# Four query projections and four gates of a retention layer by seven products, with sums kept in PSUM

## The chip, the cores and the metric

The kernel runs on one core of one Trainium2 chip. The metric is device time in microseconds of one execution, the median of several runs. A profiled execution comes with a trace of every engine: TensorE (PE, with weight loads as PEld), VectorE (DVE), ScalarE (ACT), GpSimd (POOL), and SyncE (SP), which issues most DMAs.

## The reference

One layer of a decoder for 512 tokens and 16 learned meta tokens of width 1024: retention (4 heads, keys of 256, values of 512) and stick-breaking attention (16 heads of 64) from one projection, gated and merged, then a SwiGLU feed-forward network (FFN) of width 2816. All inputs are float32.

```python
proj = hn @ w_in
rq, rk, rv, rg, sq, sk, sv, ga, gb = jnp.split(proj, ...)
q_r = rotary(heads(rq, RET_HEADS), pos) * (RET_DK ** -0.5)
k_r = rotary(heads(rk, RET_HEADS), pos)
y_ret = head_groupnorm(retention_chunkwise(q_r, k_r, heads(rv, RET_HEADS)))
y_ret = (jax.nn.silu(rg) * merge_heads(y_ret)) @ w_ret_out
y_sb = merge_heads(stick_breaking(...)) @ w_sb_out
merged = jax.nn.sigmoid(ga) * y_ret + jax.nn.sigmoid(gb) * y_sb
h = h + rmsnorm(merged @ w_out)
a, b = jnp.split(rmsnorm(h) @ w_ffn_in, 2, axis=-1)
h = h + rmsnorm((jax.nn.silu(a) * b) @ w_ffn_out)
```

## The kernel before

**Number format.** Every operand of a product is split in two parts of the format float32r: `split` copies the rounded high part on ACT (line 104) and subtracts it from the source on DVE for the low part (line 101). A product is then three matmuls per block of 128 inputs: high by high, high by low, low by high. All matmuls are issued through `mm` (line 95), so the profile shows them under one line and they are told apart by their tiles. `hT` and `hL` are the two parts of the normalised, turned input; `wh` and `wl` those of a weight.

**Plain products.** `feat_units` (137) loads blocks of weights (1024 inputs by 128 features) and `feat_mm` (142) multiplies them: features on the partitions, tokens along the columns, 8 x 3 matmuls of 512 columns for one block. Loads go through `raw_of` (118) into four buffers `raw`; the parts lie in five pairs of buffers `wh`, `wl` (pool `wun`).

**Products by seven.** A product of two 2 x 2 block matrices can be made with seven block products in place of eight (the Strassen-Winograd scheme). The class `Tokens` (174) holds the four quarters of the input, b11 to b22, and four sums of them, t1 to t4 (tiles `th`, `tl`). `feat_quarters` (221) and `tok_quarters` (238) load a weight, make its sums s1 to s4 on POOL in tiles `st` (lines 230 and 247 to 258), and split them: `raw1` holds a11 and a12, `x` holds s2 and s3, `y` holds s1 and s4. `seven` (263) runs the products in the order a11·b11, a12·b21, s2·t2, s3·t3, s1·t1, s4·b22, a22·t4, each in a PSUM bank of its own, and adds the results on DVE in a tile `ub` in SBUF (lines 274, 277, 280, 285; the copy of line 269 is on ACT). `feat_seven` (features on the partitions, 12 matmuls of 256 columns a product) serves the FFN: 20 sets of seven after the first two column blocks, on `nT`, `nL`. `tok_seven` (tokens on the partitions, 24 matmuls of 256 columns a product) serves retention's values (`rv_proj`) and its output gate (`ret_gate`).

**PSUM.** There are eight banks of 512 columns: two tiles `pp` (`bank_p`), two `pb` (`bank_b`) and two `pa` (`bank_a`, of two banks each).

**Stages.** The attention stage with the stick-breaking heads comes first, then its output projection, then retention (from about 331 us), one head after another: `ret_qk` makes queries (plain, 2 blocks, both in one `pa` tile) and keys (two blocks, 528 columns in two pieces of 264, each block in a `pa` tile) and rotates them on DVE and ACT; `ret_scores` makes decayed scores; `ret_gate` the output gate; `ret_pv` multiplies scores by values and normalises on DVE; `ret_T` turns the result; `rv_proj` makes the next head's values; `ret_out` multiplies by `w_ret_out` and adds up in `acc`. After the last head the eight blocks of the branch gate `ga` are handled: the first three were made earlier and are loaded, blocks 3 to 7 are plain products here (line 1141), with a sigmoid (1142). `mb` is the other branch, loaded from DRAM (1128); lines 1132 and 1133 multiply `acc` by the gate and add `mb`. The tiles of `ga` lie in the space of the values, `vh` and `vl`. After the output projection (`w_out`) and the norms comes the FFN, from about 852 us, and its second product, from about 1053 us.

**Order.** In most of the kernel the order of instructions on each engine is laid out when the kernel is built, by a planner that follows a model of the times and takes what is ready, in the order of the program's text where several are. So the text below gives priorities rather than an exact order. On the chip each engine then runs its own list in order. A tile with one buffer (`ub`) makes its next user wait until the last reader is done.

Of the kernel before, what the change touches and what calls it, by code (L numbers as in the profile page):

```python
# [16 lines left out]
P = 128  # L17
NM = 16
T = 512
# [15 lines left out]
def hybrid_block(  # L35
# [105 lines left out]

    def feat_mm(dst, unit, xh, xl, kn=KD):

        wh, wl = unit
        for k in range(kn):
            mm(dst, wh[:, k, :], xh(k), start=(k == 0), stop=False)
            mm(dst, wh[:, k, :], xl(k), start=False, stop=False)
            mm(dst, wl[:, k, :], xh(k), start=False, stop=(k == kn - 1))

    def tok_mm(dst, units, xh, xl, first=True, last=True, k0=0):  # L150

        n = sum(u[0].shape[1] for u in units)
        i = 0
        for wh, wl in units:
            for kk in range(wh.shape[1]):
                k = k0 + i
                mm(dst, xh(k), wh[:, kk, :], start=(first and i == 0), stop=False)
                mm(dst, xh(k), wl[:, kk, :], start=False, stop=False)
                i += 1
                mm(dst, xl(k), wh[:, kk, :], start=False, stop=(last and i == n))  # L160

# [59 lines left out]
    def feat_quarters(src, sums, pin=False):  # L221

        raw1, raw2 = raw_of(src[:, 0:P]), raw_of(src[:, P:])
        A11, A12 = raw1[:, 0:KH, :], raw1[:, KH:KD, :]
        A21, A22 = raw2[:, 0:KH, :], raw2[:, KH:KD, :]
        x = sums.tile([P, KD, P], F32, tag="st", name="st")
        y = sums.tile([P, KD, P], F32, tag="st", name="st")
        S1, S2, S3, S4 = y[:, 0:KH, :], x[:, 0:KH, :], x[:, KH:KD, :], y[:, KH:KD, :]
        for d, p, q, op in ((S1, A21, A22, ALU.add), (S2, S1, A11, ALU.subtract), (S3, A11, A21, ALU.subtract), (S4, A12, S2, ALU.subtract)):
            ins = nc.gpsimd.tensor_tensor(d, p, q, op=op)  # L230
            if pin:
                tc.keep_in_program_order(ins)
        f, g = slice(0, KH), slice(KH, KD)
        a, b, c, d = wun_split(raw1), wun_split(x), wun_split(y), wun_split(A22)
        cut = lambda u, k: (u[0][:, k, :], u[1][:, k, :])
        return dict(a11=cut(a, f), a12=cut(a, g), s2=cut(b, f), s3=cut(b, g), s1=cut(c, f), s4=cut(c, g), a22=d)

    def tok_quarters(src, sums=None):
# [17 lines left out]
        for d, p, q, op in ((y, A11, A21, ALU.subtract), (A21, A21, A22, ALU.add), (x, A21, A11, ALU.subtract), (A12, A12, x, ALU.subtract)):  # L256
            for k in range(0, KH, 2):
                nc.gpsimd.tensor_tensor(d[:, k : k + 2], p[:, k : k + 2], q[:, k : k + 2], op=op)  # L258
        u["s2"], u["s3"], u["s1"] = wun_split(x), wun_split(y), wun_split(A21)
        u["s4"], u["a22"] = wun_split(A12), wun_split(A22)  # L260
# [35 lines left out]

    def tok_seven(u, tok, ub, **kw):


        def product(n, dst):  # L300
            a, b = PRODUCTS[n]
            xh, xl = tok.operand(b)
            wh, wl = u[a]
            for s in range(2):
                ts_ = slice(s * P, (s + 1) * P)
                tok_mm(dst[:, s * 256 : (s + 1) * 256], [(wh, wl)], lambda k: xh(k)[:, ts_], lambda k: xl(k)[:, ts_])

        one = iter([bank_p, bank_p, bank_b])
        seven(product, lambda: next(one)(), bank_a, ub, **kw)

# [610 lines left out]
    s4.tile([P, L], F32, tag="dec", name="dec", bufs=1)  # L921
    s4.tile([P, 4, 512], F32, tag="ub", name="ub", bufs=1)
    s4.tile([P, NT, DV], F32, tag="g", name="g", bufs=1)
# [19 lines left out]
    def rv_proj(h):  # L943
        u = tok_quarters(w_in[:, O_RV + DV * h : O_RV + DV * (h + 1)], s4 if h else None)
        ub = s4.tile([P, 4, 512], F32, tag="ub", name="ub", bufs=1)
        vs = s4.tile([P, L], F32, tag="rt", name="vs", bufs=RT)[:NM, :DV]
# [12 lines left out]

        tok_seven(u, tokens, ub, after=meta_part)  # L960
        vh = s4.tile([P, NT, DV], F32R, tag="vh", name="vh", bufs=1)
        vl = s4.tile([P, NT, DV], F32R, tag="vl", name="vl", bufs=1)
        for q in range(4):
            c, t = q // 2, q % 2
            dst = lambda v: v[:, 2 * t : 2 * t + 2, 256 * c : 256 * (c + 1)]
            split(dst(vh), dst(vl), ub[:, q, :].rearrange("p (a b) -> p a b", a=2))
        split(rvm[0:16, :], rvm[64:80, :], vs)
# [22 lines left out]
    def ret_qk(h):  # L990
        uq = feat_units(w_in[:, O_RQ + DK * h : O_RQ + DK * (h + 1)])
        pq = bank_a()
        for e in range(2):
            feat_mm(pq[:, e, :], uq[e], xtok, ltok)
        q = [(qk_tile(), qk_tile()) for _ in range(2)]
        idf = lambda t: t[:, :T]
        rotate(pq[:, 0, :], pq[:, 1, :], cosT[:, NM:], sinT[:, NM:], idf, [(a[:, :T], b[:, :T]) for a, b in q])
        uk = feat_units(w_in[:, O_RK + DK * h : O_RK + DK * (h + 1)])
        pks = []
        for e in range(2):  # L1000
            pk = bank_a()
            for i in range(2):
                cs = slice(264 * i, 264 * (i + 1))
                feat_mm(pk[:, i, :264], uk[e], lambda k: hT[:, k, cs], lambda k: hL[:, k, cs])
            pks.append(pk[:, :, :264])
        k = [(qk_tile(), qk_tile()) for _ in range(2)]
# [65 lines left out]
    def ret_gate(u):  # L1072
        ub = s4.tile([P, 4, 512], F32, tag="ub", name="ub", bufs=1)
        tok_seven(u, tokens, ub)
        g = s4.tile([P, NT, DV], F32, tag="g", name="g", bufs=1)
        for q in range(4):
            c, t = q // 2, q % 2
            dst = g[:, 2 * t : 2 * t + 2, 256 * c : 256 * (c + 1)]
            nc.scalar.activation(dst, ub[:, q, :].rearrange("p (a b) -> p a b", a=2), AF.Silu)
        return [g[:, i, :] for i in range(NT)]  # L1080
# [30 lines left out]
    for h in range(RH):  # L1111
# [9 lines left out]
        else:  # L1121

            gall = [s4.tile([P, 4, T], F32, tag=t, name="ga", bufs=1) for t in ("vh", "vl")]
            ga = [gall[f // 4][:, f % 4, :] for f in range(KD)]
            base = []
            for f in range(0, KD, 2):
                mb = s4.tile([P, 2, T], F32, tag="st", name="mb")
                nc.sync.dma_start(mb, mS_d[:, f : f + 2, :])
                base += [mb[:, 0, :], mb[:, 1, :]]

# [260 lines left out]
```

## Time and profile before

| | us |
|---|---|
| median of 3 runs | 1178.63 (1178.5 to 1179.28) |
| the profiled execution | 1178.72 |
| its span in the trace | 1176.9 |
| TensorE busy | 1164.9 (99%) |
| VectorE busy | 844.0 (72%) |
| ScalarE busy | 532.1 (45%) |
| GpSimd busy | 333.5 (28%) |
| granted TensorE clock, mean | 0.999 |

Times of rows are in microseconds from the start of the span. A row names line, engine, operation, tiles written and read, and a count. Matmuls are pipelined, so one's recorded duration overlaps the next; the distance from one start to the next is what a matmul takes. Idle time in brackets is that of the row's engine just before it, with what ended it.

### The profile page before, as it was taken

What the parts mean: (1) busy time and instruction counts of PE and PEld (TensorE: products, weight loads), DVE (VectorE), ACT (ScalarE), POOL (GpSimd) and SP (SyncE); (2) the same over time, 40 slices, a digit from 0 to 9 for tenths busy, and PEclk for the clock granted to TensorE, in tenths of its full rate; (3) what the DMA queues carried; (4) which work ended last, traced back from release to release, by engine and by line L of the source; (5) the groups of instructions that cost most, each with busy time, mean ns of one, the idle gap of its engine ahead of it and who ended that gap; (6) DMA issues with size and microseconds to landing.
All of it is one profiled execution on the core that took longest, in us unless ns stands there. A gap on an engine that the chain in (4) does not pass through costs nothing.

```text
span 1176.9 us, 18856 instructions
## 1 busy us (share of the span) xinstructions
PE 1164.9 (99%) x7529; PEld 1056.3 (90%) x7529; DVE 844.0 (72%) x1120; ACT 532.1 (45%) x899; POOL 333.5 (28%) x358
## 2 busy tenths in 40 slices
PE   9999999999999999999999999999999999999997
PEld 7988999988899998998899898888999999998886
DVE  7488888888577873786586567767799998773333
ACT  6476666666233434434243334335455444442321
POOL 2021112126644403320240200001356676610000
PEclk9999999999999999999999999999999999999999
DMA  7332122222641323115122434344033333353311
GB/s 235 99 99 74 62 72 64 77 77 92 194 148 60 93 90 114 55 53 154 36 82 82 133 90 134 126 160 126 19 108 108 109 108 108 108 162 101 97 36 72
DMA packets 146536, 118.25 MB, mean 100 GB/s; under 512 B 3832, under 2 KB 135168, under 8 KB 146448
## 3 DMA queue, kind: packets, MB, share of 16 engines
q1 hardware_dynamic: 145856, 115.85, 32.5%
q8 instruction: 59, 0.97, 0.4%
q10 hardware_dynamic: 592, 1.20, 0.3%
q14 instruction: 29, 0.24, 0.1%
HBM read 109.96 MB, written 7.08 MB: 99 GB/s over the span
## 4 chain that ended last, share of the span: by engine, by line
PE 92%; DVE 5%; issue 1%; ACT 1%; DMA 0%; POOL 0%; POOLq 0%; DVEq 0%; ACTq 0%
PE pp L95 41%; PE pb L95 20%; PE pa L95 20%; PE pc L95 5%; PE px L95 3%; PE pb L98 3%; DVE wl L101 1%; DVE sm L603 1%; ACT wh L104 1%; DVE sl L101 0%; DMA ysb<-in_x_dram 0%; DVE al L101 0%; DVE kl L101 0%; DVE qb L101 0%; DVE qa L101 0%
## 5 line engine op out<-in xcount | busy, mean ns | idle before, releaser
L101 DVE TENSOR_TENSOR wl<-raw,wh 128x1024 fp32r<-128x1024 f32 x196 | 260.7, 1338 | 60.3 <-ACT wh L104 59.3
L104 ACT ACTIVATE wh<-raw 128x1024 fp32r<-128x1024 f32 x194 | 195.2, 1014 | 203.4 <-PE pa L95 59.5
L95 PE MATMUL pp<-hT,wh 128*128 128x512 f32 (+1 forms) x304 | 112.0, 369 | 0.0
L95 PE MATMUL pp<-hL,wh 128*128 128x512 f32 (+1 forms) x304 | 107.7, 354 | 0.0
L95 PE MATMUL pp<-hT,wl 128*128 128x512 f32 (+1 forms) x304 | 107.6, 354 | 0.0
L258 POOL TENSOR_TENSOR st<-raw 128x512 f32<-128x512 f32 x28 | 44.4, 1608 | 170.3 <-DMA raw<-in_w_in_dram 170.3
L101 DVE TENSOR_TENSOR wl<-st,wh 128x1024 fp32r<-128x1024 f32 x54 | 75.1, 1392 | 13.1 <-ACT wh L104 12.1
L95 PE MATMUL pp<-qk,wh 128*128 128x512 f32 x256 | 80.1, 394 | 0.0
L230 POOL TENSOR_TENSOR st<-raw 128x512 f32<-128x512 f32 x40 | 61.1, 1528 | 50.3 <-DVE wl L101 50.3
L95 PE MATMUL pp<-wh,hT 128*128 128x256 f32 (+1 forms) x240 | 73.9, 309 | 0.1
L95 PE MATMUL pp<-wl,hT 128*128 128x256 f32 (+1 forms) x240 | 73.0, 305 | 0.7 <-DVE wl L101 0.4
L95 PE MATMUL pp<-wh,hL 128*128 128x256 f32 (+1 forms) x240 | 73.0, 305 | 0.2 <-DVE hL L101 0.2
L104 ACT ACTIVATE wh<-st 128x1024 fp32r<-128x1024 f32 x54 | 56.6, 1056 | 35.6 <-PE pp L95 15.6
L95 PE MATMUL pa<-hL,wh 128*128 128x264 f32 (+1 forms) x208 | 66.2, 318 | 0.0
L95 PE MATMUL pa<-hT,wh 128*128 128x264 f32 (+1 forms) x208 | 66.2, 318 | 0.0
L95 PE MATMUL pa<-hT,wl 128*128 128x264 f32 (+1 forms) x208 | 66.1, 318 | 0.0
L603 DVE TENSOR_TENSOR_SCAN sm<-sm,mask 128x528 f32<-128x528 f32 (+1 forms) x64 | 54.8, 857 | 14.3 <-ACT sm L600 13.5
L95 PEld LDWEIGHTS pp<-hT,wl 128*128 128x128 f32 x304 | 57.2, 188 | 8.4
L613 POOL CAST mg<-sp 128x32 fp32r<-128x32 f32 x32 | 7.5, 233 | 197.6 <-DVE sp L604 153.7
L95 PEld LDWEIGHTS pp<-hT,wh 128*128 128x128 f32 x304 | 57.3, 188 | 5.8
L95 PEld LDWEIGHTS pp<-hL,wh 128*128 128x128 f32 x304 | 57.4, 189 | 5.3
L95 PEld LDWEIGHTS pp<-qk,wh 128*128 128x128 f32 x256 | 47.7, 188 | 10.7
(346 smaller groups left out, 3680.3 us busy)
## 6 DMA issues: line engine op xcount, KB each, us to landing
raw<-in_w_in_dram SPq DMA_DIRECT2D x88, 512.0 KB, 4.2
raw<-in_w_ffn_in_dram SPq DMA_DIRECT2D x44, 512.0 KB, 3.8
raw<-in_w_ffn_out_dram SPq DMA_DIRECT2D x22, 512.0 KB, 3.6
raw<-in_w_ret_out_dram SPq DMA_DIRECT2D x16, 512.0 KB, 3.4
raw<-in_w_sb_out_dram SPq DMA_DIRECT2D x8, 512.0 KB, 3.9
raw<-in_w_out_dram SPq DMA_DIRECT2D x8, 512.0 KB, 4.0
ysb<-in_x_dram SPq DMA_DIRECT2D x4, 512.0 KB, 7.1
gb_d<-go SPq DMA_DIRECT2D x8, 256.0 KB, 2.0
```

What stands on the lines that cost most here:

```text
L95: return keep(nc.tensor.matmul(*args, **kw))
L98: return keep(nc.tensor.transpose(dst, src, idn))
L101: return nc.vector.tensor_tensor(lo, src, hi.bitcast(F32), op=ALU.subtract)
L104: ins = nc.scalar.activation(hi, src, AF.Copy)
L230: ins = nc.gpsimd.tensor_tensor(d, p, q, op=op)
L258: nc.gpsimd.tensor_tensor(d[:, k : k + 2], p[:, k : k + 2], q[:, k : k + 2], op=op)
L603: nc.vector.tensor_tensor_scan(rev, rev, mask[:, r0:][:, ::-1], 0.0, op0=ALU.mult, op1=ALU.max)
L613: nc.gpsimd.tensor_copy(g[:, two, 0:NM], m)
```

## The change

Retention's queries go from two plain blocks to one set of seven in a new function `feat_chain`, with weights from `feat_quarters`; so do the gate blocks 4, 5 and 6, 7, as two sets. `feat_chain` and a rewritten `tok_seven` make the scheme's partial sums in the PSUM banks: a product continues to accumulate in the bank of an earlier one (`first=False`), after the state in between has been copied out on ACT. In `feat_chain` the first product of the keys is placed before the last product of the chain (`beside`). The four results of `tok_seven` are handed on one by one (`done`) instead of together at the end, the last straight from its bank. `ub` has three parts instead of four and also holds the queries and `mb`; the order in which `feat_quarters` and `tok_quarters` split their sums is changed, for the FFN too. The FFN keeps `seven` and `feat_seven`.

```diff
-    def feat_mm(dst, unit, xh, xl, kn=KD):
+    def feat_mm(dst, unit, xh, xl, kn=KD, first=True, **kw):
...
-            mm(dst, wh[:, k, :], xh(k), start=(k == 0), stop=False)
+            mm(dst, wh[:, k, :], xh(k), start=(first and k == 0), stop=False, **kw)
...
# feat_quarters
-        a, b, c, d = wun_split(raw1), wun_split(x), wun_split(y), wun_split(A22)
+        a, c, b, d = wun_split(raw1), wun_split(y), wun_split(x), wun_split(A22)
# tok_quarters
-            u["s2"], u["s3"], u["s1"], u["s4"] = [wun_split(a) for a in (A11, A21, A22, A12)]
+            u["s2"], u["s1"], u["s3"], u["s4"] = [wun_split(a) for a in (A11, A22, A21, A12)]
...
-        u["s2"], u["s3"], u["s1"] = wun_split(x), wun_split(y), wun_split(A21)
+        u["s2"], u["s1"], u["s3"] = wun_split(x), wun_split(A21), wun_split(y)
...
-    def tok_seven(u, tok, ub, **kw):
...
-        one = iter([bank_p, bank_p, bank_b])
-        seven(product, lambda: next(one)(), bank_a, ub, **kw)
+    def tok_seven(u, tok, ub, done, after=lambda n: None):
...
+        q11, q12, q22 = [ub[:, i, :] for i in range(3)]
+        pa = bank_a()[:, 0, :]
+        product(("a11", "b11"), pa)
+        nc.scalar.activation(q11, pa, AF.Copy)
+        pc = bank_p()
+        product(("a12", "b21"), pc, last=True)
+        after(1)
+        add(q11, pc)
+        done(0, 0, q11)
+        product(("s2", "t2"), pa, True)
+        nc.scalar.activation(q12, pa, AF.Copy)
+        pb = bank_p()
+        product(("s1", "t1"), pb)
+        nc.scalar.activation(q22, pb, AF.Copy)
+        product(("s3", "t3"), pa, True)
+        add(q22, pa)
+        done(1, 1, q22)
+        product(("s4", "b22"), pb, True, True)
+        add(q12, pb)
+        done(0, 1, q12)
+        product(("a22", "t4"), pa, True, True)
+        after(6)
+        done(1, 0, pa)
+
+    def feat_chain(u, tok, q, beside):
...
+        (q11, q12), (q21, q22) = [[q[:, e, H * t : H * (t + 1)] for t in range(2)] for e in range(2)]
+        banks["a"] = bank_a()[:, 0, :H]
+        product(("a11", "b11"), "a")
+        nc.scalar.activation(q11, banks["a"], AF.Copy)
+        banks["b"] = bank_p()[:, :H]
+        product(("s1", "t1"), "b")
+        nc.scalar.activation(q22, banks["b"], AF.Copy)
+        banks["c"] = bank_p()[:, :H]
+        product(("a12", "b21"), "c")
+        add(q11, banks["c"])
+        product(("s2", "t2"), "a", True)
+        nc.scalar.activation(q12, banks["a"], AF.Copy)
+        product(("s4", "b22"), "b", True)
+        add(q12, banks["b"])
+        product(("s3", "t3"), "a", True)
+        add(q22, banks["a"])
+        beside()
+        product(("a22", "t4"), "a", True)
+        nc.scalar.activation(q21, banks["a"], AF.Copy)
...
# rv_proj, ret_gate: split or silu of each result is now in done(), called from tok_seven
...
     def ret_qk(h):
-        uq = feat_units(w_in[:, O_RQ + DK * h : O_RQ + DK * (h + 1)])
-        pq = bank_a()
-        for e in range(2):
-            feat_mm(pq[:, e, :], uq[e], xtok, ltok)
+        uq = feat_quarters(w_in[:, O_RQ + DK * h : O_RQ + DK * (h + 1)], s4)
+        uk = feat_units(w_in[:, O_RK + DK * h : O_RK + DK * (h + 1)])
...
+        pq = s4.tile([P, 3, 512], F32, tag="ub", name="ub", bufs=1)
+        feat_chain(uq, tokens, pq, lambda: keys(0))
         q = [(qk_tile(), qk_tile()) for _ in range(2)]
         rotate(pq[:, 0, :], pq[:, 1, :], ...)
-        uk = feat_units(w_in[:, O_RK + DK * h : O_RK + DK * (h + 1)])
...
+        keys(1)
...
# branch gates after the last head
             for f in range(0, KD, 2):
-                mb = s4.tile([P, 2, T], F32, tag="st", name="mb")
+                if f >= 4:
+                    two = gall[f // 4][:, f % 4 : f % 4 + 2, :]
+                    feat_chain(feat_quarters(w_in[:, O_GA + P * f : O_GA + P * (f + 2)], s4), tokens, two, lambda: None)
+                    nc.scalar.activation(two, two, AF.Sigmoid)
+                mb = s4.tile([P, 3, T], F32, tag="ub", name="mb", bufs=1)[:, 0:2, :]
...
-                    else:
+                    elif f < 4:
                         (u,) = feat_units(w_in[:, O_GA + P * e : O_GA + P * (e + 1)])
```

More of the change, by code (lines that the diff above doesn't have):

```diff
@@ L156, in tok_mm @@
                 k = k0 + i
-                mm(dst, xh(k), wh[:, kk, :], start=(first and i == 0), stop=False)
-                mm(dst, xh(k), wl[:, kk, :], start=False, stop=False)
+                mm(dst, xh(k), wh[:, kk, :], start=(first and i == 0), stop=False, **kw)
+                mm(dst, xh(k), wl[:, kk, :], start=False, stop=False, **kw)
                 i += 1
-                mm(dst, xl(k), wh[:, kk, :], start=False, stop=(last and i == n))
+                mm(dst, xl(k), wh[:, kk, :], start=False, stop=(last and i == n), **kw)
     def rstd_of(dst, ss, eps, scale, n=P):
@@ L295, in feat_seven, with product, add @@
         seven(product, lambda: next(one)()[:, :H], lambda: bank_b().rearrange("p (a b) -> p a b", a=2), ub)
-    def tok_seven(u, tok, ub, **kw):
-        def product(n, dst):
-            a, b = PRODUCTS[n]
+    def tok_seven(u, tok, ub, done, after=lambda n: None):
+        def product(name, dst, more=False, last=False):
+            a, b = name
             xh, xl = tok.operand(b)
-            wh, wl = u[a]
             for s in range(2):
                 ts_ = slice(s * P, (s + 1) * P)
-                tok_mm(dst[:, s * 256 : (s + 1) * 256], [(wh, wl)], lambda k: xh(k)[:, ts_], lambda k: xl(k)[:, ts_])
-        one = iter([bank_p, bank_p, bank_b])
-        seven(product, lambda: next(one)(), bank_a, ub, **kw)
+                tok_mm(dst[:, s * 256 : (s + 1) * 256], [u[a]], lambda k: xh(k)[:, ts_], lambda k: xl(k)[:, ts_], first=not more and s == 0, last=True, skip_group_check=True)
+        def add(d, p):
+            nc.vector.tensor_tensor(d, p, d, op=ALU.add)
+        q11, q12, q22 = [ub[:, i, :] for i in range(3)]
[21 more added lines that the diff above has]
+        done(1, 0, pa)
@@ new lines, in feat_chain, with product, add @@
+    def feat_chain(u, tok, q, beside):
+        banks = {}
+        def product(name, bank, more=False):
+            a, b = name
+            feat_mm(banks[bank], u[a], *tok.operand(b), KH, first=not more, skip_group_check=True)
+        def add(d, p):
+            nc.vector.tensor_tensor(d, p, d, op=ALU.add)
+        (q11, q12), (q21, q22) = [[q[:, e, H * t : H * (t + 1)] for t in range(2)] for e in range(2)]
[17 more added lines that the diff above has]
+        nc.scalar.activation(q21, banks["a"], AF.Copy)
@@ L958, in meta_part, with done @@
             nc.vector.tensor_tensor(vs[:, cs], ps[0:16], vs[:, cs], op=ALU.add)
-        tok_seven(u, tokens, ub, after=meta_part)
         vh = s4.tile([P, NT, DV], F32R, tag="vh", name="vh", bufs=1)
         vl = s4.tile([P, NT, DV], F32R, tag="vl", name="vl", bufs=1)
[L963 to L966, printed above, removed]
+        def done(c, t, v):
+            dst = lambda o: o[:, 2 * t : 2 * t + 2, 256 * c : 256 * (c + 1)]
+            split(dst(vh), dst(vl), v.rearrange("p (a b) -> p a b", a=2))
+        tok_seven(u, tokens, ub, done, after=meta_part)
         split(rvm[0:16, :], rvm[64:80, :], vs)
```

37 lines of the change are left out of this document (18 added, 19 removed).

## The prediction

> **What bounds the kernel now.** I read the page's busy table, then the list of what TensorE waited for, then busy time by stage, then the chain that ended last.
>
> ```profile
> PE 1164.9 (99%) x7529; PEld 1056.3 (90%) x7529; DVE 844.0 (72%) x1120; ACT 532.1 (45%) x899; POOL 333.5 (28%) x358
> ...
> PE pb L98 <- DVE al L101: 1.6, 3, 0.7
> PE pp L760 <- DVE zeros L755: 1.5, 1, 1.5
> ...
> core 0: us, PE busy (x) PEld busy (x) DVE busy (x) ACT busy (x) POOL busy (x), PEclk, DMA share, GB/s
> 467.00:571.00 104.00, 103.92 (x690) 94.97 (x689) 73.18 (x94) 37.11 (x50) 25.82 (x20) 1.00 0.28 85
> 675.00:752.00 77.00, 77.00 (x477) 68.64 (x476) 56.81 (x82) 28.47 (x38) 4.75 (x6) 1.00 0.38 120
> 852.00:1053.00 201.00, 201.00 (x1679) 200.62 (x1678) 179.68 (x178) 95.72 (x118) 120.94 (x74) 1.00 0.38 113
> ```
>
> TensorE is never idle: its two longest waits come to 1.6 and 1.5 us in all, and the three stages (retention head 1, the end of head 3, the FFN's sevens) have none worth naming. The granted clock is 1.00 in each. So the time is the issue of matmuls, and removing some shortens it, as long as nothing that was covered comes out. DVE is the second engine: 70% busy in head 1, 89% in the FFN.
>
> What a matmul costs is its distance to the next, which the chain shows in runs.
>
> ```profile
> 355.46 16.96 PE pa L95 x96
> 372.43 1.29 PE pp L95 x11
> 373.72 5.84 PE pa L95 x48
> ...
> 892.15 2.86 PE pb L95 x24
> ...
> 902.17 2.86 PE pb L95 x24
> ```
>
> The run of 96 in head 0 is the query product (48 matmuls of 512 columns) and the first key product (48 of 264); the second key product alone takes 5.84 us. The query product therefore takes 16.96 - 5.84 = 11.12 us, 0.232 us each. In the FFN one product by seven is 7 x 12 = 84 matmuls of 256 columns, and the same place comes round in 902.17 - 892.15 = 10.02 us, 0.119 us each.
>
> **The gross saving.** Four query products and two pairs of gates (features 4, 5 and 6, 7) go from 48 matmuls of 512 columns to 84 of 256: 6 x (11.12 - 10.02) = 6.6 us. The instruction count rises by 6 x 36 = 216. The FFN's pace is the same form (weights stationary, tokens moving), so I take it as it stands.
>
> [...]
>
> **What else each set of seven adds.** Every weight sum and its split is new work on other engines:
>
> ```profile
> L230 POOL TENSOR_TENSOR st<-raw 128x512 f32<-128x512 f32 x40 | 61.1, 1528 | 50.3 <-DVE wl L101 50.3
> L230 POOL TENSOR_TENSOR st<-raw,st 128x512 f32<-128x512 f32 x20 | 44.5, 2227 | 0.0
> L230 POOL TENSOR_TENSOR st<-st,raw 128x512 f32<-128x512 f32 x20 | 26.2, 1311 | 25.8 <-issue 25.7
> L101 DVE TENSOR_TENSOR wl<-st,wh 128x1024 fp32r<-128x1024 f32 x54 | 75.1, 1392 | 13.1 <-ACT wh L104 12.1 <-PE pb L95 0.8
> L104 ACT ACTIVATE wh<-st 128x1024 fp32r<-128x1024 f32 x54 | 56.6, 1056 | 35.6 <-PE pp L95 15.6 <-PE pa L95 15.2 <-POOL st L230 1.8
> L269 ACT ACTIVATE ub<-pp 128x256 f32<-128x256 f32 x20 | 7.5, 375 | 22.7 <-DVE gt L1283 22.7
> L277 DVE TENSOR_TENSOR ub<-pp,ub 128x256 f32<-128x256 f32 x20 | 8.5, 423 | 1.8
> ```
>
> POOL: four sums, (61.1 + 44.5 + 26.2)/20 = 6.6 us, 40 us over six sets, on an engine busy 25.8 of 104 us. Splits: 3.5 units of 1024 instead of 2, so ACT 1.5 x 1.06 and DVE 1.5 x 1.39 us. Evacuation: four ACT copies and three DVE adds of 256, 1.5 and 1.3 us. Against that the eight token products lose DVE work: three adds over 1024 and one over 512 become three over 512 (the last three rows below).
>
> ```profile
> L258 POOL TENSOR_TENSOR st<-raw 128x512 f32<-128x512 f32 x28 | 44.4, 1608 | 170.3 <-DMA raw<-in_w_in_dram 170.3
> ...
> L274 DVE TENSOR_TENSOR ub<-pa,ub 128x1024 f32<-128x1024 f32 x8 | 9.7, 1211 | 0.8 <-PE pa L95 0.8
> L280 DVE TENSOR_TENSOR ub<-pb,ub 128x1024 f32<-128x1024 f32 x8 | 9.7, 1218 | 1.3 <-PE pb L95 0.9
> L285 DVE TENSOR_TENSOR ub<-pb,ub 128x512 f32<-128x512 f32 x20 | 13.6, 682 | 0.2
> ```
>
> That is 8 x (3 x 1.2 + 0.7 - 3 x 0.7) = 18 us less on DVE, about what the six sets add (6 x (2.1 + 1.3) = 20), and two more ACT copies each. None of this is on TensorE's path by itself: it costs nothing while DVE and ACT have the free 30% and 64% of head 1. The bytes loaded do not change: two blocks of 512 KB per query either way. But the first block now stays in its buffer until POOL has used it, so what stands behind it on SP's queue (keys, then the output gate) is loaded later; before, POOL's sums for the token products waited 170.3 us in all for loads (first row) without TensorE waiting, so I take nothing for it.
>
> **The new waits.** A sum kept in a bank must be copied before the next product may add to it.
>
> In the token products each copy has another product of 24 matmuls (2.86 us) in front of it, against an ACT copy of 0.6 us and possibly one 1.06 us split ahead. I take 0, at most 0.3 each.
>
> In the feature chain (s3, t3) waits for the copy of q12 behind one product of 12 (1.43 us), against 0.38 + 1.06 us. The range is 0 to 0.5 us, six times (no gain is possible here or below: there was no wait to lose). Behind the last product in the chain `a`, the second key product wants a third of the two `pa` tiles, so it waits for the copy of q21 too: 0.4 to 1.9 us, four times. What is queued behind on TensorE is everything; but before, the same place was already filled: between the two key products stand the 1.29 us of `pp` (11 matmuls of the output gate's first product) quoted above. I take 0.1 us per chain and 0.2 per key product, 1.4 us; the ends are 0 and 10.6.
>
> The gates have nothing between (s3, t3) and (a22, t4), which must wait for a DVE add of 0.42 us, perhaps behind a split of 1.4: 0.4 to 2 us twice, unless the next pair's first product fills it. And gates are themselves cover, for the last head's value products and turns:
>
> ```profile
> 719.55 4.17 PE pp L95 x18
> 723.72 2.31 PE pb L95 x10
> 726.03 3.02 PE pp L95 x13
> 729.05 2.99 PE pb L95 x13
> 732.04 1.63 PE pp L95 x7
> ...
> 732.08 0.60 ACT L1142 ACTIVATE ga<-pp 128x512 f32<-128x512 f32 x1 [6.42 <-PE pb L95]
> 744.65 1.29 DVE L1133 TENSOR_TENSOR acc<-acc,mb 128x512 f32<-128x512 f32 x2 [1.36 <-DMA mb<-mS_d]
> ```
>
> The `pp` runs are gate products laid between value products, and the first sigmoid waits until the last value product frees the `vh` and `vl` space. The chain writes its first copy there, so until 732 it can do only products that need no copy. Gate 3 (24 x 0.232) and three products of 12 are 9.9 us, where 38 x 0.232 = 8.8 us were used; enough, barely. Afterwards the cover is 2.2 us shorter. I take half of that as lost, 1.1 us; ends 0 and 4. The load of `mb` now has one buffer where it had two, so it waits on SP's queue for the gates before, and weights of the output products queue behind it. DVE waited 1.36 us for it already (last row), off TensorE's path; features 4 to 7 are merged only after four output products of 12 x 0.232 = 2.8 us, so 0.
>
> **The FFN's order.** `feat_quarters` now splits y (s1, s4) before x (s2, s3), and the FFN still uses s2 third and s1 fifth. Here x and y of one seven:
>
> ```profile
> 898.69 0.68 DVE L274 TENSOR_TENSOR ub<-pb,ub 128x512 f32<-128x512 f32 x1
> 899.29 1.21 DVE L101 TENSOR_TENSOR wl<-st,wh 128x1024 fp32r<-128x1024 f32 x1
> 900.43 0.41 DVE L277 TENSOR_TENSOR ub<-pp,ub 128x256 f32<-128x256 f32 x1
> 900.76 2.25 DVE L101 TENSOR_TENSOR wl<-st,wh 128x1024 fp32r<-128x1024 f32 x1
> ...
> 903.44 0.28 PE L95 MATMUL pb<-th,wh 128*128 128x256 f32 x1
> ...
> 908.40 1.06 ACT L104 ACTIVATE wh<-st 128x1024 fp32r<-128x1024 f32 x1 [0.45 <-POOL st L230]
> 910.50 1.46 DVE L101 TENSOR_TENSOR wl<-st,wh 128x1024 fp32r<-128x1024 f32 x1
> ...
> 913.46 0.28 PE L95 MATMUL pb<-th,wh 128*128 128x256 f32 x1
> ```
>
> x was ready at 900.50 for the product at 903.44. In y's place it is ready at 903.01, 0.4 us early; in the next seven 911.96 against 913.46, 1.5 us, and there the second split had waited for POOL's last sum, so x would come another 1.06 us later: 0.4. Two sevens show leads of 0.4; later ones should have more, since the splits of gate rows that also load DVE in the first sevens stop when their buffers are full. With 18 sevens exposed I put the loss between 0 (a lead remains) and 0.5 us each (9 us), and take 1.8: a few tenths in half of them.
>
> **Sum.** -6.6 + 1.4 + 1.1 + 1.8 = -2.3 with every wait at my value; but the order is laid out again for the new work, and gaps of this kind are all filled in the trace before. I count half of the 4.3, and get -4.4. The profiled execution took 1178.72 us (span 1176.9 and 1.8 around it), 0.1 over the median of 1178.63; 1178.7 - 4.4 gives 1174.3. With no wait at all it is 1172.0; the idle time before (3.1 us above) belongs to other stages and stays.
>
> **Rivals.**
> (1) The FFN becomes late: each x arrives about half a microsecond after its product could start. For it speak DVE's 89% and the 0.4 us leads, against it that a waiting TensorE gives the next x time. It is slower from 0.5 us a seven: 18 x 0.5 = 9 against 6.6, 1181; at 0.8, 1186.5. Chance 0.14.
> (2) The saving is swallowed: the chains' waits at their middle (5 us) leave -1.6 or less, 1177 (1176.3 to 1181). For it speaks that head 3 has no other work to lay between. Chance 0.22.
> (3) Weight loading becomes the bound. The row has 94.97 of 104 us in head 1 and 200.62 of 201 in the FFN, and the change moves matmuls from the first form to the second. A load of 128 columns takes 0.188 us; were they not overlapped, 84 would take 15.8 us, 4.7 over 11.12, six times: 28 us slower, 1207. Against it the FFN issues its 84 in 10.02 us. Chance 0.02.
>
> ```profile
> L95 PEld LDWEIGHTS pp<-qk,wh 128*128 128x128 f32 x256 | 47.7, 188 | 10.7
> ```
>
> [...] The pace of the FFN, at a full share, shows the loads overlapping here.
>
> **Numbers.** Forecast case (the saving less small waits, 1171 to 1176.2) 0.62; rival 2 0.22; rivals 1 and 3 0.16. About 0.2%, 2.4 us, is what a measurement can tell from no change. The range 1171 to 1181 leaves out a little at both ends.
>
> **What would show it.** PE x7745, POOL x382 and near 373 us busy, ACT near 560, DVE near 845; query chains 10.0 us long; FFN returns still 10.02 us (rival 1: longer, with PE waiting for DVE wl); waits of PE for ACT at the copies under 0.5 us each. I am wrong if TensorE's own waits pass 4 us in retention and FFN together.

## The result, and the profile after

The changed kernel took 1185.11 us (median of 5, 1182.19 to 1187.24) against 1178.71 us for the kernel before on the same chip: ratio 1.0054, 95% interval 1.0037 to 1.0071, so 6.4 us slower. The forecast was 1174.3 with a range up to 1181. The profiled execution took 1184.84 us with a span of 1183.1, 6.2 over the span before.

The busy table of the changed kernel's page, then its list of what TensorE waited for (total, times, longest):

```profile
PE 1163.0 (98%) x7745; PEld 1064.9 (90%) x7745; DVE 845.9 (72%) x1142; ACT 553.4 (47%) x949; POOL 379.2 (32%) x382
...
PE pa L95 <- DVE rt L1039: 4.4, 4, 2.1
...
PE pb L95 <- DVE wl L101: 1.6, 1, 1.6
...
PE pa L95 <- DVE ub L310: 1.0, 1, 1.0
PE pp L95 <- DVE wl L101: 0.9, 2, 0.5
...
PE pb L98 <- DVE yn L1128: 0.5, 1, 0.5
```

The work is what was forecast (x7745, x382, DVE 846). The first three waits are new, and so are the last one and one of the two that make 0.9 us; the kernel before had the other (0.4 us). None of the new ones is for ScalarE: the copies of the partial sums hold nothing up. One wait for the keys' rotation (L1039) comes in each head, one wait in the FFN, two at the start of retention (at 339.67 and 354.58), and the one for `yn` at 741.97, before a turn of the last head's result.

**The keys.** The longest is in head 1. Three views of the changed kernel around it: TensorE's instructions, the stretches of 4 us (first figures: length, TensorE busy; granted clock third from the end), and the chain that ended last.

```profile
488.12 0.28 PE L95 MATMUL pp<-wh,tl 128*128 128x256 f32 x1
490.54 0.35 PE L95 MATMUL pa<-wh,hT 128*128 128x256 f32 x1 [2.13 <-DVE rt L1039]
```

```profile
488.00:492.00 4.00, 1.87 (x16) 1.70 (x15) 3.92 (x6) 2.03 (x4) 0.61 (x1) 0.98 0.00 2
492.00:496.00 4.00, 4.00 (x19) 3.51 (x19) 3.51 (x6) 2.13 (x4) 0.00 (x0) 0.59 0.47 142
```

```profile
469.02 4.44 DMA raw<-in_w_in_dram
...
473.54 1.07 ACT wh L104
...
475.90 1.12 POOL st L258
...
477.05 1.07 ACT wh L104
...
479.28 2.32 DVE wl L101
481.60 0.60 DVE rt L1035
...
488.15 1.00 DVE qk L101
...
489.78 0.62 DVE rt L1039
...
490.54 4.41 PE pa L95 x24
```

Of the output gate's products two are issued early, into the `pp` banks; the next, a11·b11, goes into a `pa` tile, and that is free only when VectorE has read the keys out of it. From start to start TensorE loses 490.54 - 488.12 - 0.12 = 2.3 us; measured the same way the four heads lose 0.85, 2.3, 1.1 and 0.8, together 5.0. After the wait the granted clock is 0.59 over 4 us: the 24 matmuls take 4.41 us where a product of this size takes 2.86, some 1.6 us more. The chain reads backwards from there: key rotation, query rotation, a weight split of 2.32 us, two copies on ScalarE, a sum on GpSimd, and a load that landed at 473.46. The loads, sums and splits in it are those of the output gate's weights.

Before the change it was VectorE that waited here. VectorE in head 1 of the kernel before:

```profile
475.57 0.69 DVE L984 TENSOR_TENSOR rt<-rt 128x512 f32<-128x512 f32 x1
...
483.62 0.71 DVE L978 TENSOR_TENSOR rt<-pa,sinT 128x528 f32<-128x528 f32 x1 [4.28 <-PE pa L95]
484.25 0.70 DVE L982 TENSOR_TENSOR rt<-pa,sinT 128x528 f32<-128x528 f32 x1
```

The queries' rotation was over at 476.25, VectorE waited 4.28 us for the second key product, and its last read of the first key block began at 484.25. Now that read begins at 489.70, 5.5 us later, while TensorE begins the second key product only 1.9 us later (479.65 against 477.74).

**The FFN.** Busy time from 860 to 1040 us, before and after:

```profile
860.00:1040.00 180.00, 180.00 (x1511) 180.00 (x1510) 162.77 (x159) 83.87 (x103) 116.49 (x72) 1.00 0.36 106
```

```profile
860.00:1040.00 180.00, 178.45 (x1480) 176.88 (x1478) 157.04 (x153) 78.69 (x101) 112.67 (x69) 1.00 0.35 103
```

In the same time TensorE issues 31 matmuls fewer: 31 x 0.119 = 3.7 us. 1.6 of it is the one wait for `wl`; the rest is a new pace, as the chain of the changed kernel shows.

```profile
942.53 2.85 PE pb L95 x24
...
952.70 2.85 PE pb L95 x24
```

A set of seven comes each 10.17 us, where it was 10.02.

**The start of retention.** The chain of the changed kernel ahead of its wait of 1.0 us (start to start 1.15) at 354.58:

```profile
339.64 5.67 DMA raw<-in_w_in_dram
...
345.37 4.85 POOL st L230 x3
...
353.93 0.61 DVE ub L310
```

The query weights land at 345.31, GpSimd makes four sums of them, and the DVE add that frees the bank of a token product stands behind their splits.

The account, from start to start: -6.6 (saving) + 5.0 (keys) + 1.6 (clock) + 3.7 (FFN) + 1.15 and 0.7 (start of retention, at 354.58 and 339.67) + 0.6 (the wait for `yn`) = +6.15, of the 6.2 between the two spans.

### The profile page after: what moved, and what is told of

Same layout as the page of the kernel before. It is cut to its first block, busy times and chain, and to the rows that moved or that the text cites. A ratio compares the mean times of both kernels' runs of the same rounds, so it can differ in the third digit from the quotient of the medians.

```text
span 1183.1 us, 19411 instructions
## 1 busy us (share of the span) xinstructions
PE 1163.0 (98%) x7745; PEld 1064.9 (90%) x7745; DVE 845.9 (72%) x1142; ACT 553.4 (47%) x949; POOL 379.2 (32%) x382
## 4 chain that ended last, share of the span: by engine, by line
PE 81%; DVE 9%; issue 3%; ACT 3%; DMA 2%; POOL 2%; POOLq 0%; DVEq 0%; ACTq 0%
PE pp L95 38%; PE pb L95 18%; PE pa L95 14%; PE pc L95 5%; DVE wl L101 3%; PE px L95 3%; PE pb L98 2%; ACT wh L104 2%; DMA raw<-in_w_in_dram 2%; DVE sm L659 1%; POOL ts L196 1%; POOL st L230 1%; DVE qk L101 1%; DVE rt L1039 0%; DVE rt L1035 0%
## 5 line engine op out<-in xcount | busy, mean ns | idle before, releaser
L230 POOL TENSOR_TENSOR st<-raw 128x512 f32<-128x512 f32 x52 | 81.5, 1570 | 152.6 <-DMA raw<-in_w_in_dram 66.5
L95 PE MATMUL pp<-hT,wh 128*128 128x512 f32 (+2 forms) x320 | 112.9, 353 | 0.0
L95 PE MATMUL pp<-hT,wl 128*128 128x512 f32 (+2 forms) x320 | 108.5, 339 | 0.0
L95 PE MATMUL pp<-hL,wh 128*128 128x512 f32 (+2 forms) x320 | 108.5, 339 | 0.0
L95 PE MATMUL pp<-wl,hT 128*128 128x256 f32 (+1 forms) x304 | 91.0, 300 | 0.7 <-DVE wl L101 0.4
L95 PE MATMUL pp<-wh,hL 128*128 128x256 f32 (+1 forms) x304 | 91.3, 301 | 0.2 <-DVE hL L101 0.2
L258 POOL TENSOR_TENSOR st<-raw 128x512 f32<-128x512 f32 x28 | 45.3, 1638 | 69.4 <-DMA raw<-in_w_in_dram 64.7
L95 PEld LDWEIGHTS pp<-wl,hT 128*128 128x128 f32 x304 | 57.2, 188 | 3.9 <-DVE wl L101 1.4
L95 PEld LDWEIGHTS pp<-wh,hT 128*128 128x128 f32 x304 | 57.3, 188 | 3.3 <-DVE mix L1253 0.4
L95 PEld LDWEIGHTS pp<-wh,hL 128*128 128x128 f32 x304 | 57.3, 188 | 2.6 <-DVE hL L101 0.4
L95 PE MATMUL pa<-wh,th 128*128 128x256 f32 x192 | 54.9, 286 | 1.3 <-DVE ub L310 1.0
```

Source lines behind the costliest of these rows:

```text
L95: return keep(nc.tensor.matmul(*args, **kw))
```

## The experiments

**1. The FFN's order alone, taken out of the changed kernel.**

```diff
-        a, c, b, d = wun_split(raw1), wun_split(y), wun_split(x), wun_split(A22)
+        a = wun_split(raw1)
+        if x_first:   # set for the FFN alone
+            b, c = wun_split(x), wun_split(y)
+        else:
+            c, b = wun_split(y), wun_split(x)
+        d = wun_split(A22)
```

> The changed kernel with one edit: the FFN's weights split x before y again, retention's still y before x. Theory A (the FFN lost its lead: in the trace after, one seven waits 1.7 us for a low part and the sevens come every 10.18 us instead of 10.02): the FFN stage returns to 10.02 us a seven and the time falls by 3.5 to 4.5 us against the changed kernel, to about 1181. Rival (the FFN's sevens are slower for another reason, for example a later start or DVE falling behind from the stage before): the sevens stay near 10.18 and the time moves by under 1 us.

Measured: 1181.15 us (1177.77 to 1183.47), ratio 1.0022 (1.001 to 1.0033), 4.0 below the changed kernel. From 860 to 1040 us the profile counts x1511 again. The waits for the keys stay (3.3 us in four).

**2. The same order put into the kernel before, and nothing else.**

```diff
-        a, b, c, d = wun_split(raw1), wun_split(x), wun_split(y), wun_split(A22)
+        a, c, b, d = wun_split(raw1), wun_split(y), wun_split(x), wun_split(A22)
```

> The kernel before with one edit: y split before x in the FFN. Theory A alone: the sevens lengthen from 10.02 to about 10.18 us, with perhaps one wait of 1 to 2 us among the first, so 3 to 5 us slower than before, 1182 to 1184. Rival (the change's retention stage makes the FFN late): no change against before, within 1 us.

Measured: 1183.07 us (1182.6 to 1183.28), ratio 1.0038 (1.0025 to 1.005). This kernel from 860 to 1040 us:

```profile
860.00:1040.00 180.00, 178.52 (x1477) 176.68 (x1476) 157.40 (x151) 77.58 (x100) 113.14 (x71) 1.00 0.34 100
```

34 matmuls fewer, 4.0 us, of a difference of 4.5. One line of the change, with no seven of its own, costs more than half the saving.

**3. The bank of the token products' first result.**

```diff
 def tok_seven(u, tok, ub, done, ...):
-        pa = bank_a()[:, 0, :]
+        pa = bank_p()
...
-        pc = bank_p()
+        pc = bank_a()[:, 0, :]
```

> The changed kernel with one edit: in the token products the chain of sums lives in a pp tile and the single product a12 x b21 in a pa tile, the reverse of the change. Theory B (the output gate's first product waits for a pa tile until DVE has rotated the keys out of it; 0.9, 2.3, 1.1 and 0.8 us in the four heads, and after the longest the granted clock was at one half for 3.4 us): these four gaps go, no half clock is left in the body, and the time falls by 5 to 7 us, to about 1179. Rival (the sums in one bank wait for their own copies, whichever bank it is): the gaps move to other products and the time changes by under 2 us.

Measured: 1177.55 us (1176.75 to 1179.87), ratio 0.9996 (0.9988 to 1.0005), 7.6 below the changed kernel. TensorE's waits in this kernel:

```profile
PE pb L95 <- DVE wl L101: 1.4, 1, 1.4
PE pa L95 <- DVE rt L1039: 1.3, 2, 0.8
```

The waits for the rotation fall from 4.4 to 1.3 us, and no stretch at half clock is left. The rotation itself is as late as before (the last read of the first key block starts at 489.67 against 489.70); but a11·b11 is in `pp` now, s2·t2 goes on in its bank, and 11 of its matmuls (1.3 us) stand in front of the first product that needs a `pa` tile.

**4. Both.**

> Both edits, the FFN's order and the banks. If theories A and B are both right and independent, 9 to 11 us less than the changed kernel, 1174 to 1176, so 3 to 5 us faster than before. If either falls, no better than the better of the two alone.

Measured: 1174.56 us (1174.2 to 1175.68), ratio 0.9967 (0.9955 to 0.998): 10.6 below the changed kernel, nearly the sum of the two (4.0 + 7.6).

**5. One part of the change at a time, in the kernel before.** First the queries, with the token products and the gates left as they were:

```diff
-        uq = feat_units(w_in[:, O_RQ + ...])
-        pq = bank_a()   # two plain products
+        uq = feat_quarters(w_in[:, O_RQ + ...], s4, y_first=True)
+        pq = s4.tile([P, 4, 512], F32, tag="ub", ...)
+        feat_chain(uq, tokens, pq, lambda: keys(0))
```

> The kernel before with the queries by the chain alone: token products by the old function (first product in a pp tile, results added on DVE), plain gates, the FFN's x first. The matmuls go down by 4 x 1.1 = 4.4 us. Theory B (the output gate's first product in a pa tile made the gaps at the key rotation): with two products in pp tiles ahead of the first in pa, those gaps are under 0.5 us a head and 2.5 to 4.5 us are gained, 1174 to 1176. Rival (the later query rotation makes the gaps, whatever tile the gate starts in): gaps of 0.8 us or more in each head remain and at most 1 us is gained.

Measured: 1184.44 us (1184.12 to 1184.82), ratio 1.0051 (1.0039 to 1.0064). The old `tok_seven` has its first product in `pp`, and yet there are waits for the rotation (2.6 us in four, none over 0.9), and others of 1.8 and 1.1 us for DVE. So the queries' chain alone makes VectorE late, whichever tile the gate takes. VectorE has more to do here than in the changed kernel, though: the old token products keep their adds, and it is busy 83.28 of the 104 us from 467 to 571 where the changed kernel has 73.75. The 6.1 us by which it is slower than the kernel before are therefore no measure of the chain within the whole change.

Then the gates:

```diff
+                if f >= 4:
+                    feat_chain(feat_quarters(w_in[:, O_GA + ...], s4), tokens, two, lambda: None)
+                    nc.scalar.activation(two, two, AF.Sigmoid)
```

> The kernel before with gates 4 to 7 by two chains alone. The matmuls go down by 2.2 us. If the gates are needed as cover for the last head's value products and turns (my term of 1.1 us), about half of it is gained: 1177 to 1178. If the cover is long enough, 1176.4; if the chain's waits cost more than the saving, 1179 to 1180.

Measured: 1176.33 us (1175.61 to 1176.92), ratio 0.9982 (0.9974 to 0.9991): 2.1 us for two sets, 1.1 each, all that the count of matmuls gives.

Then the rewritten `tok_seven`, with its sums in the banks:

> The kernel before with the rewritten token products alone (sums in the banks, chain in a pa tile), plain queries and gates, the FFN's x first. The matmuls stay the same. Theory B with my reading that it takes both (a chain in pa and a late query rotation): two products in pp tiles (5.7 us) lie between the keys and the need for pa, 3.9 us were needed before, so no gap and the time within 1 us of before. Rival (the sums in the banks wait for their own copies): 2 us or more slower.

Measured: 1178.98 us (1178.51 to 1179.34), ratio 1.0005 (0.9996 to 1.0013): nothing clear of noise. Its trace has the wait of 0.5 us at the start of retention (at 339.94), with plain queries; that wait of the changed kernel belongs to the token products.

**6. Plain queries in head 0, on top of experiment 4.**

```diff
-        uq = feat_quarters(w_in[:, O_RQ + ...], s4)
+        uq = (feat_quarters if h else lambda s, _: feat_units(s))(w_in[:, O_RQ + ...], s4)
```

> Both edits (the FFN's order, the banks) and head 0's queries plain again. Head 0's chain gives 1.1 us of matmuls, and beside it stand gaps of 0.7, 0.8 and 0.6 us at 339, 353 and 359 us. If the gaps come from the chain's weights (their sums start when the load lands at 345 us, and an add waits on DVE behind their split), those at 353 and 359 go: 0.3 us less than with both edits. If they belong to the first value product with its new order, they stay: 1.1 us more.

Measured: 1173.18 us (1172.43 to 1173.56), ratio 0.9954 (0.9941 to 0.9968). The wait for `ub` at the start of retention is gone with the early sums. The median is 1.4 us below experiment 4, where 0.3 was expected. This is the fastest version found: 5.4 us by its ratio, where five sets can give 5 x 1.1 = 5.5.

**7. Two attempts at the keys' order, on the queries alone (x5).** The first key product behind the chain, so that the query rotation has both key products beside it:

```diff
-        feat_chain(uq, tokens, pq, lambda: keys(0))
+        feat_chain(uq, tokens, pq, lambda: None)
...
+        keys(0)
         keys(1)
```

> Queries by the chain alone, as in the run of that name (1184.4), with the first key product moved from before the chain's last product to behind the chain. Theory C (the last of the four results comes only after the first key product, so the queries' rotation and with it the keys' rotation run 5.8 us later on DVE, and the pa tiles come free late): the gaps of 0.65 to 1.0 us before the gate's first product in pa go, 3 us or so in all, while (a22, t4) may wait 0.5 to 1 us a head for its add; 1181 to 1183. Rival D (the chain takes a third pa tile, so that the work kept for the gap is used up between the two key products): the gaps stay, 1184 or more.

Measured: 1187.65 us (1186.28 to 1189.61), ratio 1.0078 (1.0064 to 1.0092). The waits for the rotation went from 2.6 to 2.0 us only, and new ones came, the longest at head 0's scores. The second attempt gave the chain a bank of another pair:

```diff
-        banks["a"] = bank_a()[:, 0, :H]
+        banks["a"] = bank_b()[:, :H]
```

> Queries by the chain alone, with the chain's main bank a pb tile instead of a pa tile; the first key product stays before the chain's last. Rival D: the second key product follows the first at once, the gate's first product is left over for the gap, and the gaps go; 1181 to 1182. Theory C: the tile that the gate waits for still comes free only after the keys' rotation, so the gaps shrink by no more than the work moved there (at most 2.8 us a head of cover, which would be enough if rotation is no later); if they stay at 0.6 us or more in two heads, C holds.

Measured: 1187.74 us (1187.08 to 1187.98), ratio 1.0078 (1.0065 to 1.009). The waits for the rotation grew to 6.0 us. Part of both times is clock: the traces have a stretch at half clock of 6.83 us in the first kernel and of 3.41 in the second, and the queries alone had none. Neither the place of the key product nor the pairs of banks explains why VectorE is late, and both theories fall as they stood.

**8. The changed kernel and that of experiment 1 in another execution each.**

> The changed kernel once more, for its spread (1182.2 to 1187.2 us). If the spread is made by stretches at half clock after a gap (one of 3.4 us in the first trace, worth about 1.7 us), this execution's time differs from 1184.8 by 1.7 us for each stretch more or less in its trace. Rival (loads or waits of varying length): the same stretches and other gaps.

> The changed kernel with the FFN's order restored once more: its five rounds ran from 1177.8 to 1183.5 while its trace (span 1176.0) had no stretch at half clock in the body. If half clock makes the spread, a time above 1180 shows one to three such stretches after the gaps at the key rotation, and a time near 1178 none.

Measured: 1185.66 us with waits of 1.8 and 2.3 us in heads 0 and 1 and a stretch at half clock behind the second; and 1182.09 us for experiment 1's kernel with waits of 2.3 and 2.2 us in heads 1 and 2 and a stretch at half clock behind the second, where its first profiled execution (1177.77) had 1.2 and 1.1 and none. The same wait is 1 us in one execution and 2 in another, which fits the spread of that kernel's times, 5.7 us, where those of experiment 6 spread by 1.1. Half clock alone does not make the spread: of the 4.3 us between the two executions of experiment 1's kernel, 2.25 are longer waits in heads 1 and 2 and 1.7 are the stretch, and the two executions of the changed kernel have one stretch each.

**9. GpSimd beside VectorE.** Two engines of the changed kernel in head 1, VectorE first:

```profile
479.28 2.32 DVE L101 TENSOR_TENSOR wl<-raw,wh 128x1024 fp32r<-128x1024 f32 x1
...
482.73 0.68 DVE L1036 TENSOR_TENSOR rt<-rt 128x512 f32<-128x512 f32 x1
...
485.67 1.78 DVE L1041 TENSOR_TENSOR rt<-rt 128x512 f32<-128x512 f32 x1
487.38 0.69 DVE L1034 TENSOR_TENSOR rt<-pa,cosT 128x528 f32<-128x528 f32 x1
```

```profile
476.97 3.55 POOL L258 TENSOR_TENSOR raw<-raw,st 128x512 f32<-128x512 f32 x2
485.34 3.27 POOL L258 TENSOR_TENSOR st<-raw 128x512 f32<-128x512 f32 x2 [4.82 <-DMA raw<-in_w_in_dram]
```

A subtraction of two SBUF tiles (L1036) takes 0.68 us while GpSimd rests, and an addition of the same size (L1041) 1.78 us while it runs; alone the addition takes 0.68 too, as the next kernel shows (L1045 there). The multiplication at 487.38, also beside GpSimd, has one operand in PSUM and takes its usual 0.69. Before the change both rotations read PSUM; now the queries come from `ub` in SBUF. The two splits beside GpSimd's pair of sums (until 476.97 + 3.55 = 480.52) differ: the one at 478.14 takes 1.23 us, as it does in the next kernel without these sums (476.87 there), and the one at 479.28 takes 2.32 and ends 1.08 us after the pair. The rows show that some of VectorE's instructions on SBUF take longer there, and not what decides which. The next kernel takes GpSimd's work on the output gate out; it leaves out the gate's sums, so its results are others, and only its time is of use:

```diff
 def tok_quarters(src, sums=None, skip=False):   # skip for the output gate
+        if skip:
+            u["s2"], u["s1"], u["s3"] = wun_split(A11), wun_split(A21), wun_split(A22)
+            u["s4"], u["a22"] = wun_split(A12), wun_split(A22)
+            return u
```

> The changed kernel with the weight sums of the output gate left out (six instructions of GpSimd a head; the four blocks are split as they were loaded, so the gate's numbers are others), everything else kept. Open is why VectorE comes to the keys' rotation so late in head 1. Theory E (VectorE and GpSimd in each other's way): between 471 and 488 us three of VectorE's instructions that read and write SBUF alone took 1.33, 2.32 and 1.78 us where the same forms take 0.68, 1.23 and 0.68 without GpSimd's sums beside them, 2.8 us together; without the sums they take the short times, the wait of 2.29 us before the gate's product goes under 0.6, the half clock behind it is not seen, and the median is 2 to 5 us below the changed kernel, 1180 to 1183. Theory F (the order of VectorE's list alone): the rotation waits for the copy of the chain's last product and for the splits ahead of it; the wait at 488 us stays over 1.5 us and the median within 1 us of 1185.

Measured: 1177.47 us (1177.2 to 1178.41), ratio 0.9994 (0.9985 to 1.0003), 7.6 below the changed kernel, where 2 to 5 were expected, with a spread of 1.2 us in 11 runs. No wait for the rotation is left in any head, nor a stretch at half clock; these had cost 5.0 and 1.6 us. VectorE in head 1 of this kernel:

```profile
476.87 1.23 DVE L101 TENSOR_TENSOR wl<-raw,wh 128x1024 fp32r<-128x1024 f32 x1 [0.20 <-ACT wh L104]
478.01 0.69 DVE L1039 TENSOR_TENSOR rt<-ub,sinT 128x512 f32<-128x512 f32 x1
...
482.17 0.68 DVE L1045 TENSOR_TENSOR rt<-rt 128x512 f32<-128x512 f32 x1
482.78 0.70 DVE L1038 TENSOR_TENSOR rt<-pa,cosT 128x528 f32<-128x528 f32 x1
```

The key rotation starts at 482.78 in place of 487.38. Through retention TensorE, VectorE and ScalarE have the same instructions in the same order as in the changed kernel, so the order of VectorE's list does not explain the lateness. This kernel takes away two things at once, the slowing and the wait of the splits for GpSimd's results. So the sums were put back into buffers that nothing reads:

```diff
         if skip:
+            x, y = [sums.tile([P, KH, 256], F32, tag="st", name="st") for _ in range(2)]
+            for d, p, q, op in ((y, A11, A21, ...), (x, A21, A22, ...), (x, x, A11, ...), (y, A12, x, ...)):
+                ...   # on GpSimd, in pieces as before
```

> The kernel y1 (the output gate's blocks split as loaded) with the six sums of GpSimd put back into buffers that nothing reads, so that GpSimd works beside VectorE but ScalarE and VectorE wait for none of its results. Leaving the sums out had moved the start of the keys' rotation in head 1 from 487.4 to 482.8 us after the changed kernel's start: by the rows 2.2 us of that because ScalarE's list stood behind a split that waited for a sum, and 2.2 us because VectorE's instructions beside GpSimd took 1.3 to 2.3 us in place of 0.7 to 1.2. Theory E (the contention decides): some of TensorE's waits before the gate's product come back, about 0.3 to 1.5 us in two heads or more, and the median is 1179 to 1182. Theory G (the wait for the sums decides): no wait over 0.3 us there, the median within 1 us of 1177.5.

Measured: 1188.35 us (1185.43 to 1191.2), ratio 1.0087 (1.0074 to 1.0101), worse than either expectation. Its waits for the rotation, and VectorE's three splits ahead of it in head 1:

```profile
PE pa L95 <- DVE rt L1047: 6.3, 4, 2.6
```

```profile
477.14 6.71 DVE L101 TENSOR_TENSOR wl<-raw,wh 128x1024 fp32r<-128x1024 f32 x3 [2.49 <-ACT wh L104]
483.77 0.68 DVE L1043 TENSOR_TENSOR rt<-ub,sinT 128x512 f32<-128x512 f32 x1
```

The three splits take 2.2 us each, where 1.23 is their time alone; their weights come straight from the loads, so none waits for a sum, and the rotation is late again. The three other engines keep the order of the kernel without the sums. Later loads are the rival, since the sums hold the `raw` buffers longer. ScalarE's copy of the block that it waits for, and its next copy, which waits for TensorE, first without the sums, then with them:

```profile
472.57 1.06 ACT L104 ACTIVATE wh<-raw 128x1024 fp32r<-128x1024 f32 x1 [4.17 <-DMA raw<-in_w_in_dram]
474.35 1.06 ACT L104 ACTIVATE wh<-raw 128x1024 fp32r<-128x1024 f32 x1 [0.71 <-PE pa L95]
```

```profile
476.05 1.06 ACT L104 ACTIVATE wh<-raw 128x1024 fp32r<-128x1024 f32 x1 [4.36 <-DMA raw<-in_w_in_dram]
477.64 1.06 ACT L104 ACTIVATE wh<-raw 128x1024 fp32r<-128x1024 f32 x1 [0.53 <-PE pa L95]
```

Against TensorE's work this load comes 0.2 us later (1.78 us between the two copies, then 1.59), while the key rotation comes 2.4 us later (482.78 and 488.52, less the 3.3 us by which TensorE is later). So GpSimd running beside VectorE is enough to bring the waits back. Its profiled execution has a span 8.1 us longer than that without the sums: the waits for the rotation (7.0 from start to start) and one stretch at half clock (1.7), less 0.4 at the start of retention, make that up. How much of the changed kernel's lateness is this and how much the wait of ScalarE's copies for the sums (2.44 us before the copy at 477.05) stays open: no run has the wait without the slowing.

**10. The FFN's pace.** The changed kernel's VectorE, GpSimd and ScalarE in one set of seven:

```profile
957.07 1.41 DVE L101 TENSOR_TENSOR wl<-st,wh 128x1024 fp32r<-128x1024 f32 x1
...
964.99 1.23 DVE L101 TENSOR_TENSOR wl<-st,wh 128x1024 fp32r<-128x1024 f32 x1
...
967.26 1.41 DVE L101 TENSOR_TENSOR wl<-st,wh 128x1024 fp32r<-128x1024 f32 x1
```

```profile
958.62 1.30 POOL L230 TENSOR_TENSOR st<-st,raw 128x512 f32<-128x512 f32 x1 [1.22 <-issue]
...
961.58 2.28 POOL L230 TENSOR_TENSOR st<-raw,st 128x512 f32<-128x512 f32 x1
...
968.81 1.30 POOL L230 TENSOR_TENSOR st<-st,raw 128x512 f32<-128x512 f32 x1 [1.22 <-issue]
```

```profile
963.89 2.01 ACT L104 ACTIVATE wh<-st 128x1024 fp32r<-128x1024 f32 x2 [0.69 <-POOL st L230]
```

VectorE finishes x at 957.07 + 1.41 = 958.48; 0.14 later GpSimd writes the next s2 into the same tile `st`, its last sum ends at 963.86, ScalarE copies y and then x, VectorE does y, two adds, and x until 968.67. That is a loop of 10.19 us through one buffer (958.48 to 968.67), longer than TensorE's 10.02. To break it, s2 and s3 got half tiles of their own with three buffers, the order of the splits kept; y keeps a buffer to itself:

```diff
-        x = sums.tile([P, KD, P], F32, tag="st", name="st")
+        S2, S3 = [sums.tile([P, KH, P], F32, tag="sx", name="sx", bufs=3) for _ in range(2)]
...
+            split(b[0][:, f, :], b[1][:, f, :], S2)
+            split(b[0][:, g, :], b[1][:, g, :], S3)
...
-    sst = s6c.enter_context(tc.tile_pool(name="sst", bufs=2, ...))
+    sst = s6c.enter_context(tc.tile_pool(name="sst", bufs=1, ...))
```

> The changed kernel with s2 and s3 of the FFN in half tiles of their own, three buffers for the two, split one after the other; the order of the splits (y before x) is kept. Theory L (a loop through the buffer st: GpSimd may write the next s2 only when VectorE has read this x, then three sums of 5.2 us, two copies on ScalarE and the splits on VectorE come round in 10.18 us): with a buffer free for the next s2 the loop is shorter by one sum of 1.3 us, and the sevens come each 10.02 us as before the change; the first wait of about 1.7 us may stay; the median is 2 to 3 us below the changed kernel. Theory M (VectorE's list alone makes x late, whatever buffer is free): the sevens stay at 10.15 us or more and the median within 1 us of 1185.

Measured: 1180.67 us (1178.54 to 1182.68), ratio 1.0016 (1.0007 to 1.0025), 4.4 below the changed kernel. From 860 to 1040 us:

```profile
860.00:1040.00 180.00, 180.00 (x1511) 180.00 (x1510) 168.84 (x173) 83.04 (x121) 113.28 (x72) 1.00 0.35 104
```

The full pace, with y still before x and VectorE busier than in either kernel (168.84 us against 162.77 and 157.04): the buffer held it, not VectorE's load. GpSimd now begins the next s2 at 952.38, while VectorE is still splitting this s2 and s3 (951.98 to 954.55). The first wait of 1.6 us went as well, which was not expected.

## Why the prediction was wrong

- **The gross saving** was right: 1.1 us a set, by the gates alone and by the five sets of experiment 6.
- **Token products, 0**: right within noise; experiment 5 gives 1.0005, with one wait of 0.5 us.
- **The feature chain, 1.4 us for all its waits**: this step failed most. Its copies cost TensorE nothing. The wait came one place later, at the output gate's first product, and cost 5.0 us and 1.6 of clock. I asked who needs the chain's banks, and not when the queries' rotation could begin. In head 1 it was over at 476.25 before and is over at 487.45 now: it stands after the chain's last copy instead of beside the first key product, it reads SBUF beside GpSimd, and the key rotation stands behind it on VectorE. The change also moved the gate's first product from `pp` to `pa`, which I had read in the diff and did not price; that exposed the lateness (experiment 3).
- **The loads, "I take nothing"**: failed at the start of retention, where the chain of the wait at 354.58 begins with a load. My row showed that GpSimd's waits for loads had been harmless; the sums of the queries have no such slack. The chain of head 1 begins with a load too, but without the gate's sums the loads are there and the wait is not.
- **New work on DVE and POOL "costs nothing while they have the free 30%"**: failed. The shares add up as forecast, but beside GpSimd single instructions of VectorE on SBUF took up to 1.78 us in place of 0.68 (experiment 9), which a sum of busy times does not show.
- **The FFN's order, 1.8 us**: it measured 3.7 here, 4.0 alone. I took a lead of 0.4 us for a static margin that would recover when the gate splits stop. The lateness closed a loop, and the whole stage took the loop's pace. Rival 1 had this mechanism at 0.5 us a seven; it was about 0.15.
- **The gates' cover, 1.1 us**: nothing by the gates alone; the changed kernel's profile has 0.6 us of it (the wait for `yn`), its second profile none.
- **"I count half of the 4.3"**: no row carried that. The waits summed to three times the 4.3. The sign that I gave for being wrong, waits over 4 us in retention and FFN, is what came: 4.4 + 1.6 + 1.0 + 0.5 + 0.5. The terms' own upper ends (10.6, 4 and 9 against 6.6) reach 17 us slower; the range stopped at 1181, which no row carried, and the measured time lies between the two.

## What to carry to other kernels

When a product is replaced, follow its consumer as well as its banks: ask when the next engine may begin, what stands behind it in its list, and which tile the following product takes. An order of splits that leaves "a few tenths" of lead in a pipeline is to be checked as a loop: from the last reader of each buffer round to the same reader again, against the pace of the bound engine. Elementwise work moved from PSUM to SBUF is to be priced beside GpSimd, not alone: here an addition took 1.78 us in place of 0.68.

## What the runs showed of the hardware

**VectorE beside GpSimd.** In the changed kernel's retention stage the rotation's instructions with an operand in PSUM take 0.69 to 0.70 us, also beside GpSimd (at 382.16 and 487.38). Those on SBUF alone take 0.67 to 0.70 us while it rests; beside it four took 0.99 to 1.78 (at 471.02, 485.67, 577.88 and 681.75) and three no more than 0.71 (at 365.17, 381.56 and 592.18).

**The clock after a short wait.** After most waits of 2 us and over in these profiles the granted clock was half for 3.41 us (once, after 2.0 us in the first kernel of experiment 7, for twice that). In the changed kernel the wait was 2.3 us (rows above); with the chain in another bank it was 2.6 us in head 0:

```profile
382.00:386.00 4.00, 1.56 (x13) 1.35 (x12) 4.00 (x7) 2.48 (x5) 0.00 (x0) 0.99 0.16 44
386.00:390.00 4.00, 3.97 (x20) 3.84 (x21) 4.00 (x5) 0.90 (x1) 2.22 (x1) 0.58 0.65 216
```

Of the nine waits of 2.0 us and over that I counted in these profiles' retention stages, seven were followed by such a stretch; none of 1.8 us or less was. A wait of 2.8 us that ended at 597.5 in the last kernel of experiment 9 was not:

```profile
597.00:601.00 4.00, 3.45 (x27) 3.28 (x28) 4.00 (x6) 2.41 (x4) 0.00 (x0) 1.00 0.15 37
```

No run shows what sets the length of a stretch, or why two of the nine waits went without one.
